# A gated mixer block in float32 on one core: first stage without Pool work, down projection with tokens on the partitions, head norms one step later

## The chip, the core and the metric

The kernel runs on one NeuronCore of one Trainium2 chip. Its engines are PE (TensorE, the matrix unit; PEld is its weight load), DVE (VectorE), ACT (ScalarE), POOL (GpSimd) and SP (SyncE, which issues most of the DMAs). The metric is the device time of one execution in microseconds. Before the change the median of three runs is 1719.18 us (1718.71 to 1719.59). The profiled execution took 1719.31 us, of which 1717.6 us is the span from its first to its last instruction; the 1.7 us around the span are not in the trace.

## The reference, cut to what matters

All is in float32, with 16 meta tokens ahead of 256 tokens, 2048 channels and one layer.

```python
h = rms_norm(x, norm_pre_mix)                       # over 2048 channels, 272 tokens
q, k, v, o, ip, fp, cb, cc, cx, pu, gates = split(h @ w_in)
y_a = mlstm(q, k, v, ip, fp, o, head_gain)          # 8 heads x 128; each head's output is normed,
                                                    # times head_gain, times sigmoid(o)
y_b = cb * causal_dwconv3(cc * cx)
y_c = multiscale_pool(pu, pool_w, pool_scale)       # 4 groups of 256 channels
merged = sum_n sigmoid(gate_n) * (y_n @ w_branch[n])
x = x + rms_norm(merged @ w_out, norm_post_mix)
h = rms_norm(x, norm_pre_ffn)
a, u = split(h @ w_ffn_in)                          # 5632 + 5632 columns
ff = (gelu(causal_dwconv3(a)) * u) @ w_ffn_out      # 5632 -> 2048, the down projection
x = x + rms_norm(ff, norm_post_ffn)                 # the norm runs over the 2048 channels of a token
return x[16:]
```

## The kernel before

**Layout and precision.** Channels lie on the 128 partitions and tokens along the free dimension. A weight is a row of 128 x 128 tiles in the order in which PE uses them (class `Weights`). SP loads 16 tiles (a 1 MB chunk, three buffers) per DMA; ACT rounds 8 tiles (a "half") to fp32r (`whi`, L84) and DVE takes the rest (`wlo`, L87); four buffers hold split halves. A product is then three fp32r matmuls: hi x hi, hi x lo and lo x hi (`gemm`, L175 to L177). `pair_step` (L183, L184) joins the two that share `whi`: one matmul of 512 columns (256 tokens, hi and lo side by side) and one of 256 columns with `wlo`, so two matmuls a tile.

**What orders the work.** Each engine runs its queue in order; the queue is laid out when the program is built, from the order of the code and the scheduler's own estimate. An instruction that waits holds back all that stand behind it on its engine.

**First stage** (`first_steps`, L230). For each of 16 channel tiles k: `xgh`/`xgl` are the two parts of x times the gain (ACT L214, DVE L215), and PE adds 12 matmuls of 272 columns into four accumulators. Four times, `square` (L218) squares four tiles and adds them up: on POOL (L222) for g = 0 and 1, on ACT (L224) for g = 2 and 3, the two levels of sums always on POOL (L225, L227). Four fp32 matmuls against `ones` (L236) then add over the partitions, and `rsqrt` gives `rstd`.

**Heads and convolutions.** After the eight heads, `norms` makes one factor per head and token (DVE and ACT, ending with L279). `conv(c)`, c = 0 to 7, runs three matmul groups of the convolution branch; between its first and its second stands `finish(c)`: a matmul that spreads the factor of head c over the partitions (L407) and DVE and ACT steps that write that head's `y0h`, `y0l`.

**Down projection and end.** For each of 16 output tiles m, 44 `pair_step`s over the 44 channel tiles of `act`; the last m uses three 256-column matmuls a tile instead (`gemm`). ACT and DVE evict the accumulator, square it and apply the gain; POOL sums the squares. Then `rsqrt` over [128 x 256], and eleven pieces that are multiplied by `r3` (L686), added to x (L688, in part on POOL) and stored.

Of the kernel before, what the change touches and what calls it, by code (L numbers as in the profile page):

```python
# [100 lines left out]


def build(tc, nc, x_d, c_d, k_d, w_d, out_d, n_tiles):
    ctx = ExitStack()
    with ctx:
# [555 lines left out]
        dn = last.tile([P, NK, SEQ], F32, name="dn", bufs=1)
        sqa = last.tile([P, SEQ], F32, name="sqd", bufs=1)
        r3 = last.tile([P, SEQ], F32, name="r3", bufs=1)
        tot = auxt()[:, 0:SEQ]
        for m in range(NK):
            if m < NK - 1:
                o = acc()
                for k in range(NF):
                    pair_step(o, ("w_ffn_out", k, m * P), act[:, k], k, NF)
                u = last.tile([P, SEQ], F32, name="du", tag="du")  # L670
                nc.scalar.copy(out=u, in_=o[:, SEQ:])
                nc.vector.tensor_tensor(out=u, in0=o[:, 0:SEQ], in1=u, op=ALU.add)
            else:
                u, = gemm([lambda k: ("w_ffn_out", k, m * P)], lambda k: act[:, k, 0], lambda k: act[:, k, 1], NF, 0, SEQ)
# [83 lines left out]
```

## Time and profile before

| | |
|---|---|
| profiled execution, its span | 1719.31 us, 1717.6 us |
| median of three runs | 1719.18 us |
| busy share of the span: PE, PEld, DVE, ACT, POOL | 98%, 94%, 59%, 47%, 11% |
| chain that ended last: PE, DVE, ACT, DMA | 94%, 4%, 1%, 1% |
| mean granted TensorE clock | 0.993 |
| HBM read, written | 302.47 MB, 2.10 MB |

A busy share is an average over the whole span. The granted clock is a share of 2.4 GHz (1.00), and 0.50 is the level of 1.2 GHz. Matmuls overlap, so their cost is read from the distance between starts and not from the length of a row. The end of a wait names the engine whose instruction released it.

### The profile page before, as it was taken

The numbers are of one execution on the slowest core, as the hardware profiler recorded it, in microseconds if no ns is written. First come the engines' busy times: TensorE is split into PE (matmuls) and PEld (weight loads), VectorE is DVE, ScalarE is ACT, GpSimd is POOL, SyncE is SP. The second block draws the span as 40 slices with busy tenths as digits, with TensorE's granted clock in tenths as the row PEclk, the third lists the DMA queues.
The fourth block names the chain that finished last, engine by engine and source line by source line (L and its number), as shares of the span: only waits on it lengthen the run. The fifth ranks groups of instructions, "written<-read, shape, count | busy, mean of one in ns | idle before, by whom it ended". The sixth has DMA issues, their size and how long they took to land.

```text
span 1717.6 us, 29764 instructions
## 1 busy us (share of the span) xinstructions
PE 1682.1 (98%) x12581; PEld 1613.4 (94%) x12581; DVE 1014.9 (59%) x1306; ACT 806.4 (47%) x1094; POOL 190.3 (11%) x211
## 2 busy tenths in 40 slices
PE   8999999999999999999999999999999999999995
PEld 7999999999999999999998899999999999888885
DVE  7655557666555555555544976666666666444444
ACT  5655555444444444444444554444444444444441
POOL 4000011110000000000022610111111110000001
PEclk9999999999999999999999999999999999999998
DMA  6544444455454555545553454545555555555551
GB/s 238 189 149 164 157 151 174 169 195 187 182 186 183 185 184 181 188 179 190 176 192 148 152 192 175 194 179 189 181 187 186 182 191 177 196 182 186 196 175 71
DMA packets 45256, 306.48 MB, mean 178 GB/s; under 512 B 5019, under 2 KB 6555, under 8 KB 8899
## 3 DMA queue, kind: packets, MB, share of 16 engines
q1 hardware_dynamic: 44978, 304.47, 49.1%
q8 instruction: 98, 1.61, 0.4%
q14 instruction: 36, 0.29, 0.0%
q10 hardware_dynamic: 144, 0.12, 0.0%
HBM read 302.47 MB, written 2.10 MB: 177 GB/s over the span
## 4 chain that ended last, share of the span: by engine, by line
PE 94%; DVE 4%; ACT 1%; DMA 1%; issue 1%; SPq 0%; POOL 0%; ACTq 0%; POOLq 0%; DVEq 0%
PE acc L183 18%; PE acc L175 17%; PE acc L176 17%; PE acc L177 17%; PE acc L184 9%; PE acc L606 5%; PE acc L605 5%; PE acc L607 5%; DVE wlo L87 1%; DMA wraw<-weights 1%; DVE dn L686 1%; DVE xs L586 1%; DVE mix L579 1%; ACT whi L84 0%; PE auxt L347 0%
## 5 line engine op out<-in xcount | busy, mean ns | idle before, releaser
L87 DVE TENSOR_TENSOR wlo<-wraw,whi 128x1024 fp32r<-128x1024 f32 (+1 forms) x573 | 708.6, 1237 | 540.8 <-ACT whi L84 539.6
L84 ACT CAST whi<-wraw 128x1024 fp32r<-128x1024 f32 (+1 forms) x573 | 599.3, 1047 | 784.1 <-PE acc L176 372.2
L175 PE MATMUL acc<-xgh,whi 128*128 128x258 f32 (+4 forms) x1776 | 505.2, 285 | 0.0
L176 PE MATMUL acc<-xgl,whi 128*128 128x258 f32 (+4 forms) x1776 | 504.1, 284 | 0.0
L177 PE MATMUL acc<-xgh,wlo 128*128 128x258 f32 (+4 forms) x1776 | 501.5, 283 | 0.0
L177 PEld LDWEIGHTS acc<-xgh,wlo 128*128 128x128 f32 x1776 | 334.6, 188 | 0.0
L176 PEld LDWEIGHTS acc<-xgl,whi 128*128 128x128 f32 x1776 | 334.7, 188 | 0.0
L175 PEld LDWEIGHTS acc<-xgh,whi 128*128 128x128 f32 x1776 | 334.2, 188 | 0.0
L183 PE MATMUL acc<-xs,whi 128*128 128x512 f32 x704 | 253.2, 399 | 0.0
L183 PE MATMUL acc<-act,whi 128*128 128x512 f32 x660 | 231.8, 393 | 0.0
L184 PE MATMUL acc<-xs,wlo 128*128 128x256 f32 x704 | 197.2, 280 | 0.0
L184 PE MATMUL acc<-act,wlo 128*128 128x256 f32 x660 | 186.7, 283 | 0.0
L606 PE MATMUL acc<-xs,whi 128*128 128x258 f32 x656 | 186.0, 284 | 0.0
L605 PE MATMUL acc<-xs,whi 128*128 128x258 f32 x656 | 185.3, 283 | 0.0
L607 PE MATMUL acc<-xs,wlo 128*128 128x258 f32 x656 | 184.2, 281 | 0.0
L183 PEld LDWEIGHTS acc<-xs,whi 128*128 128x128 f32 x704 | 133.1, 189 | 28.1
L183 PEld LDWEIGHTS acc<-act,whi 128*128 128x128 f32 x660 | 123.9, 188 | 28.6
L184 PEld LDWEIGHTS acc<-xs,wlo 128*128 128x128 f32 x704 | 134.1, 191 | 0.0
L605 PEld LDWEIGHTS acc<-xs,whi 128*128 128x128 f32 x656 | 123.3, 188 | 1.8
L607 PEld LDWEIGHTS acc<-xs,wlo 128*128 128x128 f32 x656 | 125.0, 191 | 0.0
L184 PEld LDWEIGHTS acc<-act,wlo 128*128 128x128 f32 x660 | 124.1, 188 | 0.0
L606 PEld LDWEIGHTS acc<-xs,whi 128*128 128x128 f32 x656 | 124.0, 189 | 0.0
(249 smaller groups left out, 1966.9 us busy)
## 6 DMA issues: line engine op xcount, KB each, us to landing
wraw<-weights SPq DMA_DIRECT2D x283, 1024.0 KB, 4.8
wraw<-weights SPq DMA_DIRECT2D x4, 512.0 KB, 6.8
out_t<-dn SPq DMA_DIRECT2D x5, 256.0 KB, 2.0
x<-x_t SPq DMA_DIRECT2D x4, 272.0 KB, 6.3
wraw<-weights SPq DMA_DIRECT2D x4, 256.0 KB, 5.6
out_t<-dn SPq DMA_DIRECT2D x6, 128.0 KB, 1.8
x<-x_t SPq DMA_DIRECT2D x4, 136.0 KB, 5.4
x<-x_t SPq DMA_DIRECT2D x1, 544.0 KB, 9.1
```

The source lines that it names most:

```text
L84: copied = self.nc.scalar.copy(out=hi[:, j:j + n], in_=src[:, j:j + n])
L87: self.nc.vector.tensor_tensor(out=lo[:, j:j + n], in0=src[:, j:j + n], in1=hi[:, j:j + n].bitcast(F32), op=ALU.subtract)
L175: nc.tensor.matmul(o, lhsT=wh, rhs=rh, start=k == 0, stop=False)
L176: nc.tensor.matmul(o, lhsT=wh, rhs=rl, start=False, stop=False)
L177: nc.tensor.matmul(o, lhsT=wl, rhs=rh, start=False, stop=k == nk - 1)
L183: nc.tensor.matmul(o, lhsT=wh, rhs=both, start=k == 0, stop=False)
L184: nc.tensor.matmul(o[:, 0:SEQ], lhsT=wl, rhs=both[:, 0], start=False, stop=k == nk - 1)
L579: nc.vector.tensor_tensor(out=mix[:, k], in0=mix[:, k], in1=r1, op=ALU.mult)
L586: nc.vector.scalar_tensor_tensor(out=xs[:, k, 1], in0=xk, scalar=col(C_GPRE2 + k), in1=xs[:, k, 0].bitcast(F32), op0=ALU.mult, op1=ALU.sub ...
L605: nc.tensor.matmul(o, lhsT=wh, rhs=xs[:, k, 0], start=k == 0, stop=False)
L606: nc.tensor.matmul(o, lhsT=wh, rhs=xs[:, k, 1], start=False, stop=False)
L607: nc.tensor.matmul(o, lhsT=wl, rhs=xs[:, k, 0], start=False, stop=k == NK - 1)
```

## The change

1. **First stage.** All four squares are made by ACT (`square`), and the sums by DVE (`add`, three of 128 x 1088, then 544 and 272 columns). One fp32 matmul against `ones` takes the place of four. POOL has no work left there.
2. **Heads' norms.** `finish(0)` is called in `conv(1)`, `finish(1)` in `conv(2)` and so on; `conv(7)` calls `finish(6)` and `finish(7)`.
3. **Down projection.** The stationary operand is now `act` (128 tokens), the moving one is 512 columns of weights (four tiles, `wide`). For each group of 512 output channels (four), each channel tile k and each half h of the tokens: three matmuls of 512 columns. Two accumulators are filled at once, and eight tiles (one half of a chunk) serve twelve matmuls. The gain comes as a 1 MB tile by a DMA of its own in the first group. ACT's square adds up along the free dimension (`accum_out`), so a token's sum is [128 x 1]; most of the norm is made before the last group. At the end PE transposes x (32 tiles of 128 x 128), and eight DVE instructions of 512 columns multiply, add from PSUM and are stored one by one.

Line numbers of the changed kernel are 7 higher from L100 on, and more further down. On DVE's queue in the first stage before, from the channel tiles 6 and 7 to the norm (L87 is `wlo`, L215 `xgl`, L156 the first step of `rsqrt`):

```order
L215 SCALAR_TENSOR_TENSOR xgl<-x,cst,xgh 128x272 x2
L87 TENSOR_TENSOR wlo<-wraw,whi 128x1024
L215 SCALAR_TENSOR_TENSOR xgl<-x,cst,xgh 128x272 x2
L87 TENSOR_TENSOR wlo<-wraw,whi 128x1024
L215 SCALAR_TENSOR_TENSOR xgl<-x,cst,xgh 128x272 x2
L87 TENSOR_TENSOR wlo<-wraw,whi 128x1024
L215 SCALAR_TENSOR_TENSOR xgl<-x,cst,xgh 128x272 x4
L87 TENSOR_TENSOR wlo<-wraw,whi 128x1024 x2
L156 TENSOR_SCALAR vx<-auxt 128x272
```

The same stretch of DVE's queue in the changed kernel (L223 is `xgl`, L232 and L242 are the sums of squares):

```order
L223 SCALAR_TENSOR_TENSOR xgl<-x,cst,xgh 128x272 x2
L232 TENSOR_TENSOR sums<-sums,sq 128x1088
L87 TENSOR_TENSOR wlo<-wraw,whi 128x1024
L223 SCALAR_TENSOR_TENSOR xgl<-x,cst,xgh 128x272 x2
L87 TENSOR_TENSOR wlo<-wraw,whi 128x1024
L223 SCALAR_TENSOR_TENSOR xgl<-x,cst,xgh 128x272 x2
L232 TENSOR_TENSOR sums<-sums,sq 128x1088
L87 TENSOR_TENSOR wlo<-wraw,whi 128x1024
L223 SCALAR_TENSOR_TENSOR xgl<-x,cst,xgh 128x272 x4
L232 TENSOR_TENSOR sums<-sums,sq 128x1088
L242 TENSOR_TENSOR sums<-sums 128x544
L242 TENSOR_TENSOR sums<-sums 128x272
```

The sums stand in front of the `wlo` of the next half. All five stand ahead of the `wlo` of the last two halves (tiles 12 to 15), the row that comes next.

On PE's queue before, after the twelfth of the sixteen channel tiles (L236 is the matmul against `ones`):

```order
L177 MATMUL auxt<-xgh,wlo 128x272
L236 MATMUL auxt<-sqs,ones 128x272 x3
L175 MATMUL auxt<-xgh,whi 128x272
L176 MATMUL auxt<-xgl,whi 128x272
L175 MATMUL acc<-xgh,whi 128x272
L176 MATMUL acc<-xgl,whi 128x272
L175 MATMUL acc<-xgh,whi 128x272
L176 MATMUL acc<-xgl,whi 128x272
L175 MATMUL auxt<-xgh,whi 128x272
L176 MATMUL auxt<-xgl,whi 128x272
L236 MATMUL auxt<-sqs,ones 128x272
```

The same place on PE in the changed kernel:

```order
L184 MATMUL auxt<-xgh,wlo 128x272
L243 MATMUL auxt<-sums,ones 128x272
L182 MATMUL auxt<-xgh,whi 128x272
L183 MATMUL auxt<-xgl,whi 128x272
L182 MATMUL acc<-xgh,whi 128x272
```

The one matmul that is left stands where the first three stood: behind 144 of the stage's 192 matmuls, and ahead of the other 48.

At the end of DVE's queue before, behind the last `wlo` (L156 to L160 are the norm, L686 the product with it, L688 the sum with x):

```order
L87 TENSOR_TENSOR wlo<-wraw,whi 128x1024 x2
L156 TENSOR_SCALAR vd<-auxt 128x256
L158 TENSOR_TENSOR zd<-yd 128x256
L159 SCALAR_TENSOR_TENSOR zd<-zd,vd 128x256
L160 SCALAR_TENSOR_TENSOR r_15787<-zd,yd 128x256
L686 TENSOR_TENSOR dn<-dn,r_15787 128x256
L686 TENSOR_TENSOR dn<-dn,r_15787 128x512
L688 TENSOR_TENSOR dn<-dn,x 128x256
```

The end of DVE's queue in the changed kernel (L681 evicts, L694 to L698 are the norm, L728 is product and sum in one):

```order
L87 TENSOR_TENSOR wlo<-wraw,whi 128x1024 x18
L681 TENSOR_TENSOR dn<-acc,gain 128x512
L694 SCALAR_TENSOR_TENSOR n_v<-ss,n_most 128x1
L696 TENSOR_TENSOR n_z<-n_y 128x1
L697 SCALAR_TENSOR_TENSOR n_z<-n_z,n_v 128x1
L698 SCALAR_TENSOR_TENSOR n_r<-n_z,n_y 128x1
L728 SCALAR_TENSOR_TENSOR dn<-dn,n_r,acc 128x512
L681 TENSOR_TENSOR dn<-acc,gain 128x512
L694 SCALAR_TENSOR_TENSOR n_v<-ss,n_most 128x1
L696 TENSOR_TENSOR n_z<-n_y 128x1
L728 SCALAR_TENSOR_TENSOR dn<-dn,n_r,auxt 128x512
L697 SCALAR_TENSOR_TENSOR n_z<-n_z,n_v 128x1
```

The norm is now of 128 x 1, the two halves of the tokens are interleaved, and the second half's eviction stands behind the first product of the first half. Six more rows of L728 and one of L698 follow. All transposes of x stand on PE behind the last matmul of the down projection.

The diff, cut to its core:

```diff
@@ class Weights
+    def wide(self, sources):
+        j, n = self.at % HALF, len(sources)
+        for s in sources:
+            self.tile(s)
+        return [part[:, j:j + n, :].rearrange("p n c -> p (n c)") for part in self.parts[(self.at - 1) // HALF]]
@@ first stage
+        sums = start.tile([P, 4, L], F32, name="sums", bufs=1)
         def square(g):
-            sq = start.tile([P, 4, L], F32, name="sq", tag="sq")
-            xk = x[:, 4 * g:4 * g + 4]
-            if g < 2:
-                nc.gpsimd.tensor_tensor(out=sq, in0=xk, in1=xk, op=ALU.mult)
-            else:
-                nc.scalar.activation(out=sq, in_=xk, func=AF.Square)
-            nc.gpsimd.tensor_tensor(out=sq[:, 0:2], in0=sq[:, 0:2], in1=sq[:, 2:4], op=ALU.add)
-            sqs = start.tile([P, L], F32, name="sqs", tag="sqs", bufs=4)
-            nc.gpsimd.tensor_tensor(out=sqs, in0=sq[:, 0], in1=sq[:, 1], op=ALU.add)
-            squares.append(sqs)
+            sq = sums if g == 0 else start.tile([P, 4, L], F32, name="sq", tag="sq")
+            nc.scalar.activation(out=sq, in_=x[:, 4 * g:4 * g + 4], func=AF.Square)
+            squares.append(sq)
+
+        def add(g):
+            nc.vector.tensor_tensor(out=sums, in0=sums, in1=squares[g], op=ALU.add)
...
+            if k in (9, 13, 15):
+                add((k - 5) // 4 if k < 15 else 3)
             if k == 15:
-                for g, sqs in enumerate(squares):
-                    nc.tensor.matmul(tot[:, 0:L], lhsT=ones, rhs=sqs, start=g == 0, stop=g == 3)
+                for n in (2, 1):
+                    nc.vector.tensor_tensor(out=sums[:, 0:n], in0=sums[:, 0:n], in1=sums[:, n:2 * n], op=ALU.add)
+                nc.tensor.matmul(tot[:, 0:L], lhsT=ones, rhs=sums[:, 0], start=True, stop=True)
@@ conv(c)
-            finish(c)
+            for h in [[], [0], [1], [2], [3], [4], [5], [6, 7]][c]:
+                finish(h)
@@ down projection and end
-        for m in range(NK):
...
-            sum_squares(tot, m, s, sqa)
-        rsqrt(last, r3, tot, 1.0 / D, SEQ, "d")
...
-            eng.tensor_tensor(out=dn[:, m], in0=dn[:, m], in1=x[:, m, META:], op=ALU.add)
-            nc.sync.dma_start(out=out_d[:, m, :], in_=dn[:, m])
+        def evict(h, g, o):
+            sq = last.tile([P, WIDE], F32, name="sq", tag="sq")
+            nc.scalar.activation(out=sq, in_=o, func=AF.Square, accum_out=ss[:, h, g:g + 1])
+            cols = slice(g * WIDE, (g + 1) * WIDE)
+            nc.vector.tensor_tensor(out=dn[:, h, cols], in0=o, in1=gain[:, cols], op=ALU.mult)
...
+        for g in range(NG):
+            outs = [acc() for _ in range(2)]
+            for k0 in range(0, NF, 2):
+                if g == 0 and k0 == 12:
+                    nc.sync.dma_start(out=gain, in_=g_d)
+                w = [W.wide([("w_ffn_out", k, (g * WIDE // P + i) * P) for i in range(WIDE // P)]) for k in (k0, k0 + 1)]
+                for h, o in enumerate(outs):
+                    for k, (wh, wl) in zip((k0, k0 + 1), w):
+                        ah, al = (act[:, k, i, h * P:(h + 1) * P] for i in range(2))
+                        nc.tensor.matmul(o, lhsT=ah, rhs=wh, start=k == 0, stop=False)
+                        nc.tensor.matmul(o, lhsT=al, rhs=wh, start=False, stop=False)
+                        nc.tensor.matmul(o, lhsT=ah, rhs=wl, start=False, stop=k == NF - 1)
+            for h, o in enumerate(outs):
+                evict(h, g, o)
+                if g == NG - 2:
+                    norm_most(h)
...
+        for h in range(2):
+            for g in range(NG):
+                xt = auxt() if g % 2 else acc()
+                for i in range(WIDE // P):
+                    nc.tensor.transpose(out=xt[:, i * P:(i + 1) * P],
+                                        in_=x[:, g * WIDE // P + i, META + h * P:META + (h + 1) * P], identity=ident)
+                cols = slice(g * WIDE, (g + 1) * WIDE)
+                nc.vector.scalar_tensor_tensor(out=dn[:, h, cols], in0=dn[:, h, cols], scalar=r3[:, h:h + 1], in1=xt,
+                                               op0=ALU.mult, op1=ALU.add)
+                nc.sync.dma_start(out=out_d[h * P:(h + 1) * P, cols], in_=dn[:, h, cols])
```

## Rows read from the trace of the kernel before

**Rows 1.** Busy time by stage: stretch, length, five engines, granted clock, DMA share, GB/s

```profile
6.00:41.00 35.00, 29.52 (x202) 27.71 (x203) 29.76 (x33) 20.98 (x32) 16.09 (x11) 0.95 0.72 257
1451.00:1698.60 247.60, 247.60 (x1456) 218.93 (x1454) 110.23 (x103) 106.57 (x133) 10.45 (x15) 1.00 0.47 172
1698.60:1717.60 19.00, 1.07 (x4) 0.30 (x2) 13.98 (x21) 1.64 (x4) 6.33 (x5) 0.60 0.30 111
```

**Rows 2.** Waits: who waited for whom, us in total, times, longest

```profile
PE auxt L177 <- DVE wlo L87: 4.8, 4, 2.6
...
ACT whi L84 <- PE acc L183: 160.9, 102, 1.8
```

**Rows 3.** First stage in order of time, PE: start, us, instruction, idle before

```profile
5.98 0.39 PE L175 MATMUL auxt<-xgh,whi 128*128 128x272 f32 x1 [0.29 <-ACT xgh L214]
10.90 0.39 PE L175 MATMUL auxt<-xgh,whi 128*128 128x272 f32 x1 [0.25 <-ACT whi L84]
19.36 0.43 PE L177 MATMUL auxt<-xgh,wlo 128*128 128x272 f32 x1 [2.58 <-DVE wlo L87]
32.99 1.54 PE L236 MATMUL auxt<-sqs,ones 128*128 128x272 f32 x6
36.33 0.29 PE L175 MATMUL auxt<-xgh,whi 128*128 128x272 f32 x1
40.85 0.28 PE L175 MATMUL acc<-xgh,whi 128*128 128x258 f32 x1
```

**Rows 4.** First stage in order of time, DVE and then POOL

```profile
11.58 2.36 DVE L87 TENSOR_TENSOR wlo<-wraw,whi 128x1024 fp32r<-128x1024 f32 x1
13.87 3.17 DVE L215 SCALAR_TENSOR_TENSOR xgl<-x,cst,xgh 128x272 fp32r<-128x272 f32 x2
26.98 0.90 DVE L215 SCALAR_TENSOR_TENSOR xgl<-x,cst,xgh 128x272 fp32r<-128x272 f32 x2
27.81 1.21 DVE L87 TENSOR_TENSOR wlo<-wraw,whi 128x1024 fp32r<-128x1024 f32 x1
...
9.29 2.07 POOL L222 TENSOR_TENSOR sq<-x 128x1088 f32<-128x1088 f32 x1 [6.82 <-DMA wraw<-weights]
24.77 0.85 POOL L227 TENSOR_TENSOR sqs<-sq 128x272 f32<-128x272 f32 x1
```

**Rows 5.** First stage, the stretch at the lower granted clock

```profile
20.00:21.00 1.00, 1.00 (x7) 1.00 (x6) 1.00 (x2) 1.00 (x4) 1.00 (x1) 0.50 0.94 393
```

**Rows 6.** ACT by shape: busy us, mean ns

```profile
L224 ACT ACTIVATE sq<-x 128x1088 f32<-128x1088 f32 x2 | 2.2, 1092 | 0.0
L84 ACT CAST whi<-wraw 128x512 fp32r<-128x512 f32 x2 | 1.2, 618 | 4.2 <-DMA wraw<-weights 4.2
```

**Rows 7.** In order of time, the first head and the first `conv`

```profile
50.63 0.43 DVE L279 TENSOR_TENSOR gp<-gm,gp 8x272 fp32r<-8x272 f32 x1
53.02 0.39 PE L332 MATMUL auxt<-gp,sel 128*128 128x258 f32 x1
54.07 0.53 PE L350 MATMUL auxt<-ident,vT 128*128 128x128 f32 x3
...
273.72 0.39 PE L407 MATMUL auxt<-norm,sel 128*128 128x258 f32 x1 [1.66 <-DVE norm L279]
```

**Rows 8.** Down projection in order of time, PE

```profile
1450.98 0.39 PE L183 MATMUL acc<-act,whi 128*128 128x512 f32 x1
...
1682.72 0.27 PE L175 MATMUL acc<-act,whi 128*128 128x256 f32 x1
...
1698.38 0.59 PE L553 MATMUL auxt<-sqd,ones 128*128 128x256 f32 x2
```

**Rows 9.** The last DVE instruction, and two shapes of DVE's

```profile
1713.76 0.69 DVE L688 TENSOR_TENSOR dn<-dn,x 128x512 f32<-128x512 f32 x1
...
L335 DVE TENSOR_SCALAR e<-auxt,aT 128x16 f32<-128x16 f32 x8 | 1.8, 227 | 0.0
L87 DVE TENSOR_TENSOR wlo<-wraw,whi 128x512 fp32r<-128x512 f32 x2 | 1.4, 692 | 6.9 <-ACT whi L84 6.9
```

More of the change, by code (lines that the diff above doesn't have):

```diff
@@ L660, in build @@
         last = ctx.enter_context(tc.tile_pool(name="last", bufs=2, reuse_waits="tile"))
[L661 to L664, printed above, removed]
-        for m in range(NK):
[L666 to L674, printed above, removed]
-            s = sqa if m == 0 else last.tile([P, SEQ], F32, name="sq", tag="sq")
-            nc.scalar.activation(out=s, in_=u, func=AF.Square)
-            nc.scalar.activation(out=dn[:, m], in_=u, func=AF.Copy, scale=col(C_GPOST2 + m))
-            if m == 1:
-                ln_exp_tables()
-            sum_squares(tot, m, s, sqa)
@@ L681, in build @@
[L681 to L689 removed]
+        WIDE = 512
@@ new lines, in build @@
+        NG = D // WIDE
+        gain = last.tile([P, D], F32, name="gain", bufs=1)
+        dn = last.tile([P, 2, D], F32, name="dn", bufs=1)
+        ss = last.tile([P, 2, NG], F32, name="ss", bufs=1)
+        most, v, y, z, r3 = (last.tile([P, 2], F32, name=f"n_{n}", bufs=1) for n in ("most", "v", "y", "z", "r"))
+        def evict(h, g, o):
[3 more added lines that the diff above has]
+            nc.vector.tensor_tensor(out=dn[:, h, cols], in0=o, in1=gain[:, cols], op=ALU.mult)
@@ new lines, in norm_most, with norm @@
+        def norm_most(h):
+            m = most[:, h:h + 1]
+            nc.vector.tensor_tensor(out=m, in0=ss[:, h, 0:1], in1=ss[:, h, 1:2], op=ALU.add)
+            for g in range(2, NG - 1):
+                nc.vector.tensor_tensor(out=m, in0=m, in1=ss[:, h, g:g + 1], op=ALU.add)
+            nc.vector.tensor_scalar(out=m, in0=m, scalar1=1.0 / D, scalar2=EPS, op0=ALU.mult, op1=ALU.add)
+        def norm(h):
+            m, t, vv, yy, zz = most[:, h:h + 1], ss[:, h, NG - 1:], v[:, h:h + 1], y[:, h:h + 1], z[:, h:h + 1]
+            nc.scalar.activation(out=yy, in_=t, func=AF.Ln, scale=1.0 / D, bias=m)
+            nc.vector.scalar_tensor_tensor(out=vv, in0=t, scalar=1.0 / D, in1=m, op0=ALU.mult, op1=ALU.add)
+            nc.scalar.activation(out=yy, in_=yy, func=AF.Exp, scale=-0.5)
+            nc.vector.tensor_tensor(out=zz, in0=yy, in1=yy, op=ALU.mult)
+            nc.vector.scalar_tensor_tensor(out=zz, in0=zz, scalar=-0.5, in1=vv, op0=ALU.mult, op1=ALU.mult)
+            nc.vector.scalar_tensor_tensor(out=r3[:, h:h + 1], in0=zz, scalar=1.5, in1=yy, op0=ALU.add, op1=ALU.mult)
@@ new lines, in build @@
+        for g in range(NG):
[14 more added lines that the diff above has]
+                    norm_most(h)
+            if g == 0:
+                ln_exp_tables()
@@ new lines, in build @@
+        for h in range(2):
+            norm(h)
+        for h in range(2):
+            for g in range(NG):
[7 more added lines that the diff above has]
+                nc.sync.dma_start(out=out_d[h * P:(h + 1) * P, cols], in_=dn[:, h, cols])
@@ L710 @@
     w_d = dram("weights", (N_TILES // CHUNK, P, CHUNK, P))
-    out_d = dram("out_t", (P, NK, SEQ), "ExternalOutput")
+    g_d = dram("gain", (P, D))
+    out_d = dram("out_t", (SEQ, D), "ExternalOutput")
     with tile.TileContext(nc) as tc:
-        order = build(tc, nc, x_d, c_d, k_d, w_d, out_d, N_TILES)
+        order = build(tc, nc, x_d, c_d, k_d, g_d, w_d, out_d, N_TILES)
     assert len(order) == N_TILES
@@ L752 @@
         units[32 + h, P + h * P:P + (h + 1) * P] = 1.0
-    arrays = {"x_t": xt, "consts": cst, "units": units, "weights": weights}
+    gain = np.ascontiguousarray(np.broadcast_to(a["norm_post_ffn"].reshape(1, D), (P, D)))
+    arrays = {"x_t": xt, "consts": cst, "units": units, "gain": gain, "weights": weights}
     r = run_bass_kernel_spmd(nc, [arrays], core_ids=[0])
     out = r.results[0]["out_t"]
-    return np.ascontiguousarray(out.transpose(2, 1, 0).reshape(1, SEQ, D))
+    return out.reshape(1, SEQ, D)
```

8 lines of the change are left out of this document (1 added, 7 removed).

## The prediction

> **What bounds the kernel now.** Read the busy time by stage first [rows 1]. In the down projection PE is busy 247.60 of 247.60 us at granted clock 1.00. There only a cheaper stream of matmuls helps, not a shorter wait. Two stretches are different: the first stage, where PE works 29.52 of 35.00 us at a mean granted clock of 0.95, and the end, where PE works 1.07 of 19.00 us. Then read the waits [rows 2]: four waits of PE for DVE's `wlo` make 4.8 us, all in the first stage.
>
> The rows in order of time say why. While POOL works (9.29 to 25.62 [rows 4]), a `wlo` of 1024 columns takes 2.36 us and two `xgl` take 3.17; just after, the same take 1.21 and 0.90 [rows 4]. After the longest wait (2.58 us, until 19.36) a matmul row lasts 0.43 instead of 0.29 us [rows 3] and the granted clock is at the level of 1.2 GHz [rows 5]. The mean of 0.95 over 35 us [rows 1] prices that fall at 35 x 0.05 = 1.75 us.
>
> **The change, part by part.** All sums are made against the profiled execution (span 1717.6, 1719.3 with what lies around it); the median of the runs is 0.1 less.
>
> *First stage.* Before, the first matmul starts at 5.98 and the next stage's at 40.85: 34.9 us [rows 3]. Thirty-six matmuls of 272 columns lie between 36.33 and 40.85, so 0.1256 us each [rows 3]; the 192 of the stage need 24.1. The four fp32 matmuls against `ones` are eight rows of (1.54 - 0.39) / 5 = 0.23 us [rows 3], 1.8 us; two rows are left, 0.46.
>
> Now the new order. PE begins the third and fourth channel tile at 10.90 before, having done 24 matmuls (3.0 us), so 1.9 us are lost by then, to data and to ACT's cast [rows 3]. That stays. ACT's first square now stands ahead of that cast: 1.09 us [rows 6], so the cast ends about 11.7 instead of 10.85 and PE loses 0.8 more. From 11.7 I follow DVE's queue up to the last sum: five `wlo` at 1.21, twelve `xgl` at 0.45, three sums of 1088 columns (not in the trace; 1.21 x 1088 / 1024 = 1.29 from the `wlo`), two of 0.64 and 0.32: 6.05 + 5.4 + 3.87 + 0.96 = 16.3, so 28.0. PE comes to the matmul against `ones` after 144 matmuls: 5.98 + 18.1 + 1.9 + 0.8 + some 0.3 for a late `wlo` = 27.1. So PE, with 48 matmuls queued behind, waits 0.9 us for the sums; DVE's queue sets this stage. Then 28.0 + 0.46 + 48 x 0.1256 = 34.5. The `wlo` of the last two halves come at 29.2 and 30.4, before PE needs them (29.5 and 31.5). No wait is longer than 1.3 us, so I assume that the clock stays up. The stage ends at 34.5 for 40.85: **-6.4 us**. Bounds: -7.1, if the DVE rows overlap so far that PE never waits at `ones` except for 0.2; -3.5, if the clock falls again (+1.75) and ACT makes DVE wait for another 1.1.
>
> The stage after it gets less slack. Before, `gp` is there at 50.63 + 0.43 = 51.06 and PE uses it at 53.02 [rows 7], 12.2 us after the stage's end. Everything in between waits for PE to free weight buffers, since ACT's small steps stand among its casts. I put 0.5 us for a new wait there, between 0 and 1: **+0.5 us**.
>
> *Heads' norms.* The first `finish` makes PE wait 1.66 us for the norm's last step [rows 7]. With `conv(0)` calling none, a whole `conv` of matmuls lies in between; that hides it. The last `conv` gets two, one matmul more, and the first user of `y0h[7]` comes behind 48 x 3 matmuls of gates, some 17 us later: **-1.7 us**, between -1.0 and -1.7.
>
> *Down projection.* Columns first: before 704 tiles x 768, now 4 x 44 x 2 x 3 = 1056 matmuls x 512, both 540,672. What changes is their form. Before, 660 pairs lie between 1450.98 and 1682.72, 0.3511 us a pair, and 132 matmuls of 256 columns between there and 1698.38, 0.1186 each [rows 8]. So one of 512 costs 0.2325, and 1056 cost 245.5 for 247.4: **-1.9 us**. Bare streams of 512 are not in the trace. Below, 512 columns at 2.4 GHz are 0.2133 us (-22); above, if the 256 of the pair took only its columns' 0.1067, the 512 takes 0.2444 (+10.7). I take the value from the rows, since the two forms were timed next to each other.
>
> The Trainium skill prices it in "TensorE: Matmul & The Clock Gate", section "Back-to-back issue gap": columns / 2.4 plus 2.5 ns for a matmul. That would be 215.8 + 109.2 = 325 ns for the pair, and the rows show 351, so the rule does not hold here; by its fixed part alone the 396 matmuls fewer would save 1.0 us, near the 1.9 above.
>
> Weight supply: ACT waits for PE to release a split buffer in 102 casts (160.9 us in total [rows 2]), so the splitting has time to spare, and a half still lasts 12 x 0.2325 = 2.8 us on PE as eight pairs did. The 1 MB of gain is one DMA at a mean DMA share of 0.47 [rows 1], ahead of weights that are three buffers early; ACT and DVE have the two evictions of each group to do within 61 us. Nothing of that reaches PE.
>
> *End.* Before, the last matmul of the projection hands over at 1698.4 and the span ends at 1717.6, 19.2 us; DVE's last instruction ends at 1714.45 [rows 9], so storing the last piece takes 3.15. After, call the hand-over T. The first half's accumulator is done six matmuls (1.4 us) earlier; its square (0.62, as a cast of 512 columns [rows 6]) and product (0.69, as a 512-column DVE row [rows 9]) fit ahead of T. From T on DVE has eight instructions of 512 columns at 0.69, the other half's product at 0.69, and eight of one column at 0.23 (the row of 16 columns [rows 9], the nearest): 5.5 + 0.7 + 1.8 = 8.0; with 3.15 for the last store T + 11.3 (with 0.1 for the hand-over). 19.2 - 11.3: **-7.9 us**. Bounds: -9.1 if one-column instructions take half, -6 if a store of 256 KB every 0.7 us queues or the transposes are late. The transposes: three take 0.53 us in the heads, the last row's 0.27 included, 0.13 apart [rows 7], so 0.52 for four, under the 0.69 of the DVE instruction they feed.
>
> The Trainium skill speaks against that last cover. "TensorE: Matmul & The Clock Gate", section "PE-mode transpose", says that transposes do not count as work for the clock. In the end of this trace, where PE hardly works, the mean granted clock is 0.60 [rows 1]. By that rule four transposes could come to 1.04 us, 8.3 for all, and the end would be about 1.2 us later, inside the bound above.
>
> **Sum.** -6.4 + 0.5 - 1.7 - 1.9 - 7.9 = -17.4, so 1719.3 - 17.4 = 1701.9 us.
>
> **Rivals.**
>
> *A. The first stage gains little.* POOL's work went, but 4.8 us of sums and two squares more now stand in DVE's and ACT's queues. If casts, squares and sums wait for one another in turn and the clock falls again, the stage ends near 39 instead of 34.5: 1706.5. For it: DVE's queue sets the stage in my own sum. Against: ACT has 14 us free in these 35 [rows 1]. 17%.
>
> *B. The 512-column stream runs at the clock.* If the excess over 0.2133 comes from changing between the forms, the projection takes 225.3 and the time is 1682. For it: the granted clock is 1.00. Against: streams of 256 alone are 0.1186 for 0.1067, no nearer to the clock. The page's rule on the gap says this. 3%.
>
> *C. Slower.* In the projection all eight tiles of a half are held through twelve matmuls, and the first `wlo` is wanted at the third. If PE waits w for each of the 88 halves, the time grows by 88 w. From w = 17.4 / 88 = 0.20 us on the kernel is slower; at w = 0.3 it is 1728. For it: cast and `wlo` need 2.3 us of a half's 2.8. Against: they run up to three halves ahead, and ACT waits for PE, not PE for ACT [rows 2]. 3%.
>
> *D. The end does not shrink by half.* If the stores queue up behind one another and the small steps are bound by their hand-overs, the end takes 16 us: 1706.5. For it: ten short DVE and ACT steps in a row that no row shows. Against: with a DMA share of 0.30 the stores were mostly idle in the end before [rows 1]. 10%.
>
> **How the numbers follow.** The forecast holds 67%, with its own range of 1698 to 1705. A and D end near 1706.5; the bounds of the terms, added, are 1699 to 1711. The range of 1697 to 1708 takes in A and D and leaves out B, C and the case of A and D together. A difference of 0.2% (3.4 us) is what a measurement of this kernel can tell from none. All of the forecast, A, B and D are beyond that on the fast side: faster 0.95. C holds the slower side, 0.03, and 0.02 is left for no change.
>
> **What would show it.** Right: `wlo` near 1.2 us from the first on; no granted clock of 0.5 after 6 us; one wait of about 1 us at the matmul against `ones`; the next stage's first matmul near 34.5; no wait in front of the first `finish`; 1056 matmuls some 0.2325 us apart; a last stretch of about 11 us without PE's matmuls. Wrong: slow `wlo` without POOL (then something else, such as the incoming DMAs, slowed DVE); matmul starts of more than 0.245 us; PE waits for `wlo` in the projection; stores that land more than 4 us behind DVE's last instruction.

## The result and the profile after

The changed kernel takes 1699.81 us (median of four runs, 1699.50 to 1699.99) for 1719.14 us before (1718.71 to 1719.59). The ratio is 0.9887 with a 95% interval of 0.9870 to 0.9904: faster by 1.1%, some 19.3 us, where 17.4 were forecast. The profiled execution took 1699.5 us with a span of 1697.8; the spans differ by 19.8 us.

The stages come first, as in [rows 1] (stretch, length, the five engines' busy time, granted clock, DMA share, GB/s):

```profile
6.00:34.00 28.00, 26.34 (x195) 25.02 (x196) 25.15 (x39) 22.63 (x35) 0.32 (x1) 1.00 0.86 321
1445.00:1690.00 245.00, 245.00 (x1070) 199.13 (x1069) 110.92 (x108) 95.46 (x106) 0.00 (x0) 1.00 0.48 174
1690.00:1697.80 7.80, 0.79 (x8) 0.55 (x6) 4.21 (x9) 0.00 (x0) 0.00 (x0) 0.87 0.70 251
```

The first stage is over in 28 us, at granted clock 1.00 for 0.95, with DVE busy in 25.15 of them. In the projection PE never idles. The end is short, with the DMA share at 0.70 for 0.30.

PE and then DVE in the first stage, in order of time (start, us, instruction, idle before and what ended it), to set against [rows 3, 4]:

```profile
6.24 0.39 PE L182 MATMUL auxt<-xgh,whi 128*128 128x272 f32 x1 [0.55 <-ACT xgh L222]
11.69 0.39 PE L182 MATMUL auxt<-xgh,whi 128*128 128x272 f32 x1 [1.00 <-ACT whi L84]
27.28 0.73 PE L243 MATMUL auxt<-sums,ones 128*128 128x272 f32 x2
33.88 0.28 PE L182 MATMUL acc<-xgh,whi 128*128 128x258 f32 x1
```

```profile
11.66 1.23 DVE L87 TENSOR_TENSOR wlo<-wraw,whi 128x1024 fp32r<-128x1024 f32 x1 [1.43 <-ACT whi L84]
12.81 0.91 DVE L223 SCALAR_TENSOR_TENSOR xgl<-x,cst,xgh 128x272 fp32r<-128x272 f32 x2
13.63 1.22 DVE L87 TENSOR_TENSOR wlo<-wraw,whi 128x1024 fp32r<-128x1024 f32 x1
24.71 1.29 DVE L232 TENSOR_TENSOR sums<-sums,sq 128x1088 f32<-128x1088 f32 x1
26.03 1.20 DVE L242 TENSOR_TENSOR sums<-sums 128x544 f32<-128x544 f32 x2
```

`wlo` takes 1.22 us from the first on (2.36 before). The next stage's first matmul starts at 33.88 instead of 40.85: 7.0 us. The longest wait is the 1.00 us for ACT's cast at 11.69; PE reaches the matmul against `ones` when the sums are just done: they end at 27.23 and it starts at 27.28.

What follows up to the projection: the last head's row of L394 (L387 before) starts at 252.1 instead of 259.2, still 7.1 earlier; the branches' first matmul (`yh`, L182 for L175) at 440.5 instead of 449.6, 9.1 earlier. So the heads' norms gave 2.0 us between these two, and the first `finish` comes without a wait:

```profile
288.53 0.28 PE L414 MATMUL auxt<-norm,sel 128*128 128x258 f32 x1
```

The projection in two rows of its groups (first and last start, number), against [rows 8]:

```profile
L709 PE MATMUL acc<-whi,act x352: 390/393/404, 1441.7 to 1686.4; 128*128 128x512 f32 x176
L711 PE MATMUL acc<-wlo,act x352: 390/393/404, 1442.2 to 1686.9; 128*128 128x512 f32 x176
```

The first of 1056 matmuls starts at 1441.74, the last at 1686.90: 0.2324 us apart, 245.4 in all for 247.4.

The end, DVE in order of time, to set against [rows 9] (L694 to L698 are the norm of 128 x 1, L681 the eviction of the other half, L728 product and sum):

```profile
1687.51 0.16 DVE L697 SCALAR_TENSOR_TENSOR n_z<-n_z,n_v 128x1 f32<-128x1 f32 x1
1687.98 0.75 DVE L728 SCALAR_TENSOR_TENSOR dn<-dn,n_r,acc 128x512 f32<-128x512 f32 x1
1688.64 0.68 DVE L681 TENSOR_TENSOR dn<-acc,gain 128x512 f32<-128x512 f32 x1
1689.24 0.15 DVE L694 SCALAR_TENSOR_TENSOR n_v<-ss,n_most 128x1 f32<-128x1 f32 x1
1689.31 0.15 DVE L696 TENSOR_TENSOR n_z<-n_y 128x1 f32<-128x1 f32 x1
1689.38 0.74 DVE L728 SCALAR_TENSOR_TENSOR dn<-dn,n_r,auxt 128x512 f32<-128x512 f32 x1
1693.47 0.74 DVE L728 SCALAR_TENSOR_TENSOR dn<-dn,n_r,auxt 128x512 f32<-128x512 f32 x1
```

T = 1687.13 is where the projection's last matmul hands over (0.23 us after its start). From there DVE works almost without a gap until 1694.21, T + 7.1; the span ends 3.6 us behind that. Together that is 10.7 us for 19.2.

Part of the old end bears the signs of the first stage's conflict, which the experiments below take apart. In the kernel before, POOL made five of the sums of the end (L688) beside DVE's products (L686). DVE, POOL and DVE again, in the trace of before:

```profile
1702.14 1.03 DVE L686 TENSOR_TENSOR dn<-dn,r 128x256 f32<-128x256 f32 x2
1703.25 1.37 POOL L688 TENSOR_TENSOR dn<-dn,x 128x512 f32<-128x512 f32 x1 [17.83 <-DVE dn L686]
1703.42 2.09 DVE L686 TENSOR_TENSOR dn<-dn,r 128x256 f32<-128x256 f32 x2
```

Two products, of 256 and of 512 columns, take 1.03 us before POOL's first sum and 2.09 beside it. Three more pairs and the last product are stretched in the same way; by these rows that is some 4.7 us of the old end's 19.2, an estimate. On DVE the five sums would have taken about 3.2 us by its own rows of L688 (0.69 for 512 columns, 0.41 for 256). No run separates this share of the end's gain from the rest.

The pieces add up to the span's difference: 7.1 (first stage, to the last head) + 2.0 (norms) + 0.2 (on the way) + 2.0 (projection) + 8.5 (end) = 19.8.

### The profile page after: what moved, and what is told of

Read it like the earlier page. It is cut to its first block, busy times and chain, and to the rows that moved or that the text cites. A ratio compares the mean times of both kernels' runs of the same rounds, so it can differ in the third digit from the quotient of the medians.

```text
span 1697.8 us, 28898 instructions
## 1 busy us (share of the span) xinstructions
PE 1678.4 (99%) x12207; PEld 1593.7 (94%) x12207; DVE 1002.1 (59%) x1305; ACT 796.8 (47%) x1067; POOL 157.2 (9%) x182
## 4 chain that ended last, share of the span: by engine, by line
PE 95%; DVE 3%; ACT 1%; issue 1%; DMA 0%; SPq 0%; DVEq 0%; POOL 0%; ACTq 0%; POOLq 0%
PE acc L182 17%; PE acc L183 17%; PE acc L184 17%; PE acc L190 9%; PE acc L711 5%; PE acc L709 5%; PE acc L710 5%; PE acc L614 5%; PE acc L191 5%; PE acc L613 5%; PE acc L615 5%; DVE wlo L87 1%; DVE xs L594 1%; DVE mix L587 1%; ACT whi L84 0%
## 5 line engine op out<-in xcount | busy, mean ns | idle before, releaser
L87 DVE TENSOR_TENSOR wlo<-wraw,whi 128x1024 fp32r<-128x1024 f32 (+1 forms) x573 | 705.2, 1231 | 540.4 <-ACT whi L84 539.2
L182 PE MATMUL acc<-xgh,whi 128*128 128x258 f32 (+4 forms) x1776 | 504.8, 284 | 0.0
L182 PEld LDWEIGHTS acc<-xgh,whi 128*128 128x128 f32 x1776 | 333.8, 188 | 0.0
L711 PE MATMUL acc<-wlo,act 128*128 128x512 f32 x352 | 138.9, 395 | 0.0
L710 PE MATMUL acc<-whi,act 128*128 128x512 f32 x352 | 138.9, 395 | 0.0
L709 PE MATMUL acc<-whi,act 128*128 128x512 f32 x352 | 138.9, 395 | 0.0
L650 POOL TENSOR_TENSOR fy<-fy,r 128x256 f32<-128x256 f32 x44 | 57.6, 1309 | 419.7 <-ACT fy L649 419.7
```

Of the source, the lines that this page charges most:

```text
L87: self.nc.vector.tensor_tensor(out=lo[:, j:j + n], in0=src[:, j:j + n], in1=hi[:, j:j + n].bitcast(F32), op=ALU.subtract)
L182: nc.tensor.matmul(o, lhsT=wh, rhs=rh, start=k == 0, stop=False)
L709: nc.tensor.matmul(o, lhsT=ah, rhs=wh, start=k == 0, stop=False)
L710: nc.tensor.matmul(o, lhsT=al, rhs=wh, start=False, stop=False)
```

## The experiments

All are edits of the changed kernel, whose time is 1699.8 us; each difference below is one of medians. The runs of one kernel lie within 1 us, with the one exception named. Between kernels there is a scatter of about the same size that their edits do not explain. It starts at ACT's second cast of weights, here in the changed kernel:

```profile
7.78 0.62 ACT L84 CAST whi<-wraw 128x512 fp32r<-128x512 f32 x1 [1.18 <-DMA wraw<-weights]
```

In eight kernels, the changed one among them, the first stage has the same order on PE, DVE and ACT, and in each the next stage's first matmul starts 26.07 to 26.12 us after this cast. The cast itself waits for its weights and starts anywhere between 7.11 and 8.07 us in the profiled executions. Differences below 1 us are therefore read from the traces.

**The first stage as before.**

```diff
-            sq = sums if g == 0 else start.tile([P, 4, L], F32, name="sq", tag="sq")
-            nc.scalar.activation(out=sq, in_=x[:, 4 * g:4 * g + 4], func=AF.Square)
+            if g < 2:
+                nc.gpsimd.tensor_tensor(out=sq, in0=xk, in1=xk, op=ALU.mult)
+            else:
+                nc.scalar.activation(out=sq, in_=xk, func=AF.Square)
+            nc.gpsimd.tensor_tensor(out=sq[:, 0:2], in0=sq[:, 0:2], in1=sq[:, 2:4], op=ALU.add)
...
```

> The changed kernel with the first stage as it was before (POOL makes two of the squares and all sums, four fp32 matmuls against ones), the rest as changed. Theory (the first stage's gain is real and reaches the end): POOL's work brings back wlo of 1024 columns of about 2.4 us instead of 1.22 while POOL works, PE waits for wlo of some 4.8 us in all, a stretch at granted clock 0.50, and the next stage's first matmul near 40.9 instead of 33.9. The time is then 1699.8 + 7.0 = 1706.8 us. Rival 1 (most of it is given back in the heads by new waits for weight buffers): 1702 to 1704. Rival 2 (the slow wlo came from the incoming DMAs or from the old order of the other stages): wlo stays at 1.22, time 1701 or less.

Measured: 1706.69 us, +6.9. The waits for `wlo` are back, 3.8 us in three (4.8 in four before), and so is the granted clock of 0.50, between 19 and 22 us (PE, in order of time):

```profile
18.85 0.59 PE L184 MATMUL auxt<-xgh,wlo 128*128 128x272 f32 x1 [2.58 <-DVE wlo L87]
41.10 0.28 PE L182 MATMUL acc<-xgh,whi 128*128 128x258 f32 x1
```

The theory holds; of the 7 us next to nothing is given back later.

**The heads' norms as before.**

```diff
-            for h in [[], [0], [1], [2], [3], [4], [5], [6, 7]][c]:
-                finish(h)
+            finish(c)
```

> The changed kernel with finish(c) called in conv(c) again, the rest as changed. Theory: the one wait of 1.66 us of PE for the norm comes back at the first finish and nothing else changes: 1699.8 + 1.7 = 1701.5 us. Rival 1 (the other 0.6 us that the stretch between first stage and projection gained also comes from moving the heads' norms): 1702.1. Rival 2 (with the first stage 7 us shorter DVE is no later relative to PE and the wait is hidden or longer): below 1700.3, or above 1702.5.

Measured: 1701.70 us (1701.51 to 1701.99), +1.9. The wait is back to a hundredth (PE, in order of time):

```profile
264.82 0.28 PE L183 MATMUL acc<-xgl,whi 128*128 128x258 f32 x1
266.77 0.39 PE L414 MATMUL auxt<-norm,sel 128*128 128x258 f32 x1 [1.67 <-DVE norm L286]
```

The 1.9 lies between the theory's 1.7 and the first rival's 2.3, and the stretch from the heads to the branches gave 2.0. What lies beyond the 1.67 is part of the same wait: the row counts it from the modelled end of the matmul ahead (264.82 + 0.28). From start to start the two are 1.95 us apart, and the next matmul comes 0.23 later, at 267.00, where the neighbours are 0.12 apart. That makes 1.94 us lost at this one place.

**The projection and the end as before.** The edit puts back `pair_step`, `rsqrt` over 128 x 256 and the eleven pieces.

> The changed kernel with the down projection and the end as before (tokens along the free dimension, POOL sums squares, rsqrt over 128 x 256), the rest as changed. Theory: the projection takes 247.4 instead of 245.4 us and the end 19.2 instead of 10.7: 1699.8 + 2.0 + 8.5 = 1710.3 us. Rival (the new form has a side effect on the stages ahead of it, by the weights' buffers or the gain's DMA): the three parts then do not add up, and the time is off 1710.3 by more than 0.7 either way.

Measured: 1709.82 us (1709.29 to 1710.07), +10.0. The projection starts at 1441.28 and hands over at 1688.68, again 247.4 us; the span ends at 1707.9, 19.2 later. Both lengths are as expected. The median is 0.5 below the expected 1710.3, and the projection began 0.5 earlier in the profiled execution; its second cast started 0.35 earlier. The three parts give 6.9 + 1.9 + 10.0 = 18.8 of 19.3: they add up within the scatter of four medians. The run takes back the projection and the end together; their shares, 2.0 and 8.5, come from the traces.

**Is it POOL's reading that slows DVE?** Two kernels have surplus work on POOL in the first stage. In the first one POOL reads `x` and writes a tile that nobody uses:

```diff
+            if g < 2:
+                nc.gpsimd.tensor_tensor(out=idle, in0=xk, in1=xk, op=ALU.mult)
+            nc.gpsimd.tensor_tensor(out=idle[:, 0:2], in0=xk[:, 0:2], in1=xk[:, 2:4], op=ALU.add)
+            nc.gpsimd.tensor_tensor(out=idle[:, 0], in0=xk[:, 0], in1=xk[:, 1], op=ALU.add)
```

> The changed kernel with extra work on POOL in the first stage whose result nobody uses: the ten tensor operations of before (two of 1088 columns, four of 544, four of 272, reading x and writing a scratch tile), so that POOL is busy for some 14 us while no other engine waits for it and the order on PE, DVE and ACT stays. Theory (POOL's reads slow the operations of DVE with two inputs): wlo of 1024 columns goes from 1.22 to some 2.4 us and two xgl from 0.91 to about 3.2 while POOL works, PE waits for wlo by several us, and the time rises by 5 us or more: 1705 to 1709. Rival (the slow rows of before came from the incoming DMAs or from DVE's wait for POOL's results): wlo stays at 1.22, time 1699.8 within 0.5.

Measured: 1708.60 us (1707.42 to 1710.10, a wider scatter than the others), +8.8, with no order on PE, DVE or ACT changed. DVE and then POOL in order of time:

```profile
12.15 2.34 DVE L87 TENSOR_TENSOR wlo<-wraw,whi 128x1024 fp32r<-128x1024 f32 x1
14.41 3.16 DVE L224 SCALAR_TENSOR_TENSOR xgl<-x,cst,xgh 128x272 fp32r<-128x272 f32 x2
17.50 2.36 DVE L87 TENSOR_TENSOR wlo<-wraw,whi 128x1024 fp32r<-128x1024 f32 x1
```

```profile
11.96 1.44 POOL L234 TENSOR_TENSOR idle<-x 128x544 f32<-128x544 f32 x1
13.48 1.63 POOL L235 TENSOR_TENSOR idle<-x 128x272 f32<-128x272 f32 x1
15.19 2.08 POOL L233 TENSOR_TENSOR idle<-x 128x1088 f32<-128x1088 f32 x1
22.08 0.86 POOL L235 TENSOR_TENSOR idle<-x 128x272 f32<-128x272 f32 x1
```

These are the durations of [rows 4] to a hundredth or two. Read across the two fences: `wlo` is issued at 12.15 while POOL is at work since 11.96, and lasts until 14.49, 1.1 us beyond POOL's end at 13.40, about its own 1.22. POOL's next instruction, issued at 13.48, lasts 1.63 us until 15.11, 0.6 beyond the end of that `wlo`, where the same shape can take 0.86 in all. It looks as if each waited for the other's instruction to end; the runs in the projection below test that.

In the second kernel POOL only writes:

```diff
+        for i in range(24):
+            nc.gpsimd.memset(idle, 0.0)
```

> The changed kernel with 24 fills of a scratch tile of 128 x 1088 by POOL over the first stage, which write and do not read, and which nobody waits for. Theory (the conflict needs POOL's reads, as the Trainium skill says in 'SBUF — State Buffer' of operations that read SBUF): wlo stays at 1.22 us and the time at 1699.8 within 0.5. Rival (any work of POOL slows DVE): wlo of 2 us and more while POOL fills, and the time 1704 to 1709.

Measured: 1699.62 us, no change, with POOL filling from 3.36 to 27.84 without a pause (POOL, 23 of the 24 fills, then DVE, in order of time):

```profile
3.36 24.48 POOL L222 MEMSET idle<- 128x1088 f32 x23
```

```profile
13.68 1.22 DVE L87 TENSOR_TENSOR wlo<-wraw,whi 128x1024 fp32r<-128x1024 f32 x1
```

So it is POOL's reading, not its being busy: 20.9 us of POOL's work in the stage's 28 leave `wlo` at 1.22. The rows agree with the Trainium skill, "SBUF — State Buffer", section "Who interferes with whom": an operation of DVE with two inputs in SBUF conflicts with a POOL operation that reads SBUF and not with one that only writes, and the one that comes second waits for the whole of the first.

**The same conflict in the projection.** There a half lasts 2.79 us on PE and DVE needs 1.22 of it.

```diff
+        for i in range(100):
+            nc.gpsimd.tensor_tensor(out=idle, in0=pair[0], in1=pair[1], op=ALU.add)
```

> The changed kernel with 100 extra tensor operations of POOL in the down projection (1024 columns, reading two pieces of the activations, writing a scratch tile that nobody uses), some 210 us of POOL beside the 245.4 us of PE. Theory (the supply of split weights has time to spare there, so the same conflict that cost the first stage 7 us costs nothing): wlo of 1024 columns goes from 1.22 to about 2.4 us, a half still lasts 2.79 us on PE, ACT's waits for PE shrink, PE waits nowhere, time 1699.8 within 0.5. Rival (a wlo of 2.4 us behind its cast of 1.0 us is too late, as in the slower case of the forecast): PE waits for each of some 75 halves, w = 0.1 to 0.6 us, and the time is 1707 to 1745.

Measured: 1767.65 us. The theory fell: a `wlo` took 3.33 us and not 2.4 (DVE, 1447 to 1740; then PE's wait):

```profile
L87 DVE TENSOR_TENSOR wlo<-wraw,whi 128x1024 fp32r<-128x1024 f32 x83 | 270.2, 3326 | 1.9 <-ACT whi L84 1.6 <-issue 0.3
```

```profile
PE acc L715 <- DVE wlo L87: 23.6, 73, 2.7
```

With DVE as the bound a half lasts 3.33 instead of 2.79, and the projection runs from 1441.1 to 1731.5, 290.4 us for 245.4: 45.0 more, 0.51 for each of 88 halves. That is the mechanism of the forecast's slower rival, here caused by the surplus work. The rest is the end, where POOL's surplus work itself runs on until 1765.2 and the span ends at 1765.9.

**Shorter instructions on POOL.** The 2.4 us were carried over from [rows 4]; the long ones say that it is a question of turns.

```diff
-        idle = last.tile([P, 4, SEQ], F32, name="idle", bufs=1)
+        idle = last.tile([P, 2, SEQ], F32, name="idle", bufs=1)
...
-        for i in range(100):
+        for i in range(130):
```

> The kernel with POOL's surplus work in the down projection again, now 130 operations of 512 instead of 100 of 1024 columns; nobody uses their result. Theory (DVE's and POOL's instructions take turns, so that a wlo lasts its own 1.22 us and one whole POOL instruction, which for 512 columns is about 1.0 to 1.1 us): wlo of 1024 columns lasts about 2.3 us instead of the 3.33 with POOL's longer instructions, which is less than the 2.79 us that PE takes for a half, so PE waits nowhere and the time is 1699.8 within 0.5. Rival (both get half of a common rate, whatever the length of an instruction): wlo stays near 3.3 us while POOL works, the projection is 0.5 us longer for each half, over some 60 to 75 halves 30 to 38 us, time 1730 to 1738.

Measured: 1702.18 us, +2.4, which is neither the theory's time nor the rival's; the trace tells the two apart (DVE, then POOL, 1445 to 1640 and 1690):

```profile
L87 DVE TENSOR_TENSOR wlo<-wraw,whi 128x1024 fp32r<-128x1024 f32 x70 | 127.0, 1818 | 59.4 <-ACT whi L84 58.9 <-issue 0.3
```

```profile
L703 POOL TENSOR_TENSOR idle<-act 128x512 f32<-128x512 f32 x126 | 236.0, 1873 | 9.9
```

`wlo` takes 1.82 us in the mean, from 1.22 to 2.36: the shortest is its own time alone, the longest that and 1.1 us more, about one short POOL instruction. PE waits nowhere in the projection, and its last matmul starts at 1686.15. With POOL busy almost all the time, a shared rate would have left no `wlo` at 1.22. So the two take turns by whole instructions. The 2.4 us come behind the projection: POOL worked until 1693.3, the span ends 13.9 us after the hand-over instead of 10.7 (the hand-over itself came 0.75 us earlier, 0.7 of it from the second cast on), and the small steps of the norm waited for it, while the eviction and the product beside them, which read one input from PSUM, kept their pace (DVE in order of time):

```profile
1686.77 1.20 DVE L697 SCALAR_TENSOR_TENSOR n_z<-n_z,n_v 128x1 f32<-128x1 f32 x1
1688.28 0.75 DVE L732 SCALAR_TENSOR_TENSOR dn<-dn,n_r,acc 128x512 f32<-128x512 f32 x1
1688.94 0.68 DVE L681 TENSOR_TENSOR dn<-acc,gain 128x512 f32<-128x512 f32 x1
1689.54 1.14 DVE L694 SCALAR_TENSOR_TENSOR n_v<-ss,n_most 128x1 f32<-128x1 f32 x1
```

**The price of 512 columns.**

```diff
                         nc.tensor.matmul(o, lhsT=ah, rhs=wh, start=k == 0, stop=False)
-                        nc.tensor.matmul(o, lhsT=al, rhs=wh, start=False, stop=False)
-                        nc.tensor.matmul(o, lhsT=ah, rhs=wl, start=False, stop=k == NF - 1)
+                        nc.tensor.matmul(o, lhsT=ah, rhs=wl, start=False, stop=False)
+                        nc.tensor.matmul(o, lhsT=al, rhs=wh, start=False, stop=k == NF - 1)
```

> The changed kernel with the three matmuls of each tile and half of the down projection in another order, so that the same stationary operand stands twice in a row (ah with wh, ah with wl, then al with wh). Theory (a 512-column matmul takes 0.2324 us whatever stood before it): the projection stays at 245.4 us, time 1699.8 within 0.4. Rival (what a matmul takes over the 0.2133 of its columns comes from the change of the stationary operand): a third of the changes goes, 352 x up to 0.019 = 6.7 us less: 1693 to 1697.

Measured: 1698.93 us (1698.79 to 1699.36). The first matmul starts at 1440.99 and the last hands over at 1686.39: 245.4 us, as the theory said and the rival did not. The time is 0.9 below the changed kernel's and so outside the expected 0.4. That lies ahead of the projection, which begins 0.75 earlier in this execution; 0.6 of it is there from the second cast on (7.19 for 7.78). The change of the stationary operand is not what a matmul takes beyond its columns.

**The cast ahead of the square.**

```diff
+            if g == 0:
+                tc.keep_in_program_order(done)
```

(`done` is the square; it then stands behind the cast of channel tiles 2 and 3. The orders on DVE and PE were laid out anew around it and differ in a few places.)

> The changed kernel with ACT's first square of the first stage held behind the cast of the weights of channel tiles 2 and 3, the rest as changed. Theory (the square ahead of that cast costs PE 0.75 us, which DVE's queue then carries to the stage's end): PE's wait for that cast falls from 1.00 to about 0.25 us, the next stage's first matmul comes at 33.1 instead of 33.9, time 1699.8 - 0.7 = 1699.1 us. Rival 1 (the cast waits for its data and not for ACT): no change, 1699.8. Rival 2 (what is saved there is lost again because the later xgh or the sums come later): PE's wait shrinks but the stage ends as before, 1699.8.

Measured: 1699.76 us, no change. The wait for the cast shrinks, and the time comes back as a wait for the sums (PE in order of time):

```profile
11.15 0.39 PE L182 MATMUL auxt<-xgh,whi 128*128 128x272 f32 x1 [0.26 <-ACT whi L84]
27.56 0.73 PE L245 MATMUL auxt<-sums,ones 128*128 128x272 f32 x2 [0.82 <-DVE sums L244]
34.15 0.28 PE L182 MATMUL acc<-xgh,whi 128*128 128x258 f32 x1
```

DVE on its way to the sums waits for ACT's cast:

```profile
13.90 1.23 DVE L87 TENSOR_TENSOR wlo<-wraw,whi 128x1024 fp32r<-128x1024 f32 x1 [0.43 <-ACT whi L84]
```

The second rival came: DVE's last sum is done at 27.51 with the square late and at 27.23 with it early, and the stage ends 26.17 us after the second cast, for 26.10. DVE began its first `wlo` of 1024 columns at 11.13 instead of 11.66, and then lost 0.20 and 0.43 us in waits for ACT, whose square now stood behind the cast. It is the supply by DVE and ACT that sets the stage, and not PE.

**The sums' matmul later.** This edit comes on top of the last one, with the square behind the cast.

```diff
-                nc.tensor.matmul(tot[:, 0:L], lhsT=ones, rhs=sums[:, 0], start=True, stop=True)
+                tc.keep_in_program_order(nc.tensor.matmul(tot[:, 0:L], lhsT=ones, rhs=sums[:, 0], start=True, stop=True))
```

> The kernel with the first square behind the cast, and PE's one matmul against ones behind 180 instead of 144 matmuls of the first stage, so that PE no longer waits for DVE's sums there; DVE's steps of the norm move back too. Theory (the 0.82 us that PE waits for the sums is a pure loss): PE's wait goes, the next stage's first matmul comes at 33.3 instead of 34.15, time 1699.0. Rival (DVE is the bound and the norm's factor is late instead: in the changed kernel the first head's gp was ready only 0.5 us before PE wanted it, and it comes 3 to 4 us later now): the stage's matmuls end earlier, PE waits 2 to 4 us at the first head, time 1701 to 1703.

Measured: 1700.65 us (1700.55 to 1701.06), +0.85 to the changed kernel and +0.9 to the one with the last edit alone. PE and then DVE in order of time:

```profile
28.20 0.40 PE L184 MATMUL auxt<-xgh,wlo 128*128 128x272 f32 x1 [0.81 <-DVE wlo L87]
33.78 0.28 PE L182 MATMUL acc<-xgh,whi 128*128 128x258 f32 x1
50.05 0.39 PE L341 MATMUL auxt<-gp,sel 128*128 128x258 f32 x1
54.53 0.39 PE L382 MATMUL auxt<-prh,vh 128*128 128x258 f32 x1 [0.38 <-ACT prh L170]
```

```profile
49.56 0.43 DVE L288 TENSOR_TENSOR gp<-gm,gp 8x272 fp32r<-8x272 f32 x1
```

The wait for the sums only became one of 0.81 us for the next `wlo`, behind the sums on DVE. `gp` is 3.7 us later than in the changed kernel (45.85); no wait of 2 to 4 us follows, since PE's order was laid out anew around it, but two of 0.4 us do (for one of them the profile names no releaser). The stage itself ends 26.29 us after the second cast, later than in the last kernel (26.17) and the changed one (26.10). The theory fell, and the rival has the sign and not the size.

**The stores of the end.**

```diff
+                    queue = nc.scalar if (g + j) % 2 else nc.sync
+                    queue.dma_start(out=out_d[h * P:(h + 1) * P, cols], in_=dn[:, h, cols])
```

(The last piece is also cut in two of 256 columns.)

> The changed kernel with the stores of the end issued in turn by SP and ACT, and the last product and its store cut in two of 256 columns. Theory (the last store is bound by its own issue, transfer and completion, not by the seven ahead of it): DVE's last instruction ends 0.1 us later, the last piece is half as long, and the span ends 0.2 to 0.6 us earlier: 1699.2 to 1699.6. Rival 1 (the stores queue behind one another at some 380 GB/s, so that only the sum of bytes counts): 1699.8 within 0.2. Rival 2 (ACT's queue issues later or the smaller pieces are slower): 1700.2 or more.

Measured: 1700.28 us (1699.82 to 1700.40), +0.5. DVE's last instruction ends at 1694.51 and the span at 1698.6, 4.1 us later for 3.6; the two small stores take longer to land than the large ones (size, median us from issue to landing):

```profile
out_t<-dn SPq DMA_DIRECT2D x4, 256.0 KB, 2.7
out_t<-dn ACTq DMA_DIRECT2D x3, 256.0 KB, 2.6
out_t<-dn ACTq DMA_DIRECT2D x1, 128.0 KB, 3.1
out_t<-dn SPq DMA_DIRECT2D x1, 128.0 KB, 3.0
```

The second rival came. The edit changes the queue and the size together, and why half the bytes take longer was not tried. No variant here is faster than the changed kernel by more than the scatter of the second cast.

## Why the prediction was right, step by step

The place and the mechanism of every gain were as forecast. Every term came out more favourable than forecast, by 0.6, 0.5, 0.2, 0.1 and 0.6 us in the order below. The misses all lie on one side, so they do not cancel and make up the 2.1 us between 1701.9 and 1699.8. The result is at the lower end of what the bounds of the terms allow: added, with the projection at its -1.9, they give 1699.5 to 1707.9, and not the 1699 to 1711 of the forecast.

*First stage, -6.4 forecast, -7.0 measured.* `wlo` was fast, the granted clock did not fall, and PE waited 1.00 us at the cast (0.25 + 0.8 forecast). The mis-sized step is DVE's queue: the forecast added up durations, to 28.0 for the last sum. Rows that follow at once overlap: `wlo` to `xgl` is 1.15 us from start to start for a row of 1.23, and two `xgl` take 0.82 for a row of 0.91. The last sum was done at 27.23. PE would have started the matmul against `ones` at 27.14, close to the forecast 27.1, and started it at 27.28, so that the forecast 0.9 us of waiting, one of the signs of being right, did not occur. Of the 0.7 us won there, 0.1 was lost behind it (6.60 us from that matmul to the stage's end for 6.49). DVE's queue and PE's own stream end almost together here; where PE is ahead, as with the shifted square, it waits for the sums.

*New wait at the first head, +0.5 forecast, 0 measured.* `gp` was done at 46.28 and PE used it at 46.75 without waiting. The 0.5 us was a guess between 0 and 1 that no row bears out. The cover is thin, as moving the matmul against `ones` showed.

*Heads' norms, -1.7 forecast; -2.0 by the trace, -1.9 by the run.* The forecast took the 1.66 us that the row of the wait names. From start to start the gap before was 1.94 us (271.78 to 273.72) and the next one 0.22, where the neighbours are 0.12 apart, so the place cost 1.9 us. The row counts only from the modelled end of the matmul ahead, 0.28 after its start.

*Down projection, -1.9 forecast, -2.0 measured.* 0.2324 us a matmul for 0.2325: the subtraction from [rows 8] held to a part in 2000. The rival of 512 columns at the clock would have shown 225 us. The formula that the forecast quotes from the Trainium skill ("TensorE: Matmul & The Clock Gate", section "Back-to-back issue gap") is given there for a single matmul by itself and not for a stream; it makes 0.2158 us of 512 columns, and the rows of this stream show 0.2324. The slower rival needs a `wlo` beyond 2.79 us; with POOL free it takes 1.22, and the experiment with POOL's long reads shows what the rival's price is when it does, 0.51 us a half.

*End, -7.9 forecast, -8.5 measured.* Two terms were off, in opposite directions, so that a part of this fit is luck. The eight steps of one column took 0.15 us, and 0.07 from start to start where they did not need each other, for 0.23 taken from 16 columns; the rows of 512 columns lay 0.66 apart for 0.69. That gave T + 7.1 for T + 8.0. The last store took 3.6 us for 3.15. A small row's price does not fall to nothing, but these rows of one column are a third shorter than the row of 16, which is another operation and reads PSUM. What the forecast did not see is that POOL's sums had stretched the old end, by some 4.7 us in the estimate above. It took the old end's 19.2 us as measured, so the sum does not depend on it.

*The transposes* took 0.44 us for four, 0.109 apart, and all were done by 1690.8, ahead of DVE. The 1.2 us that the Trainium skill's rule on them ("TensorE: Matmul & The Clock Gate", section "PE-mode transpose") would have added did not come; whether the rule holds, these rows can't tell, since they follow straight on a stretch at granted clock 1.00, and it stayed at 1.00 until 1690.8.

*Rivals A and D* did not come: the stage ended at 33.88 and not near 39, and the end took 10.7 us and not 16, its stores landing 2.7 us after their issue in the median.

## What to carry to other kernels

Look for POOL instructions that read SBUF beside a DVE queue that is nearly full. In these runs they delayed DVE's operations with two inputs in SBUF by whole instructions (`wlo` 2.4 us for 1.22), and a fill did no harm. What it costs depends on DVE's slack and on the length of one POOL instruction: the same kind of work cost nothing in the projection at 512 columns and 45 us at 1024. When the bound is a queue, add up distances between starts and not durations. Price a wait of PE from start to start as well: the row said 1.66 us and the place cost 1.9. Expect a wait that is taken from PE to come back at the next instruction of the queue that sets the pace.
